# A low-rank adapter's forward pass: one chunk of the input on GpSimd's DMA queue, and the chunks in another order

## The chip, the cores and the metric

The kernel runs on one core of a Trainium2 chip. The metric is the device time of one execution in microseconds, the median of several runs. A profile is one further execution, recorded by the hardware profiler.

## The reference

x has 16 x 2048 = 32,768 rows of 256 numbers in float32. W is 256 x 256, lora_A 256 x 16, lora_B 16 x 256, lora_E has 16 numbers, and scale is 1.0.

```python
x_flat = x.reshape(-1, in_dim)
y = x_flat @ W
lora_out = x_flat @ lora_A
lora_out = lora_out * lora_E
lora_out = lora_out @ lora_B
y = y + scale * lora_out
```

The input and the output have 33.55 MB each; the weights together have 0.3 MB.

## The kernel before, in words

**One weight.** The two paths have the same input, so the kernel first builds one weight, weff = W + (lora_A * lora_E * scale) @ lora_B, and then does y = x @ weff in bfloat16 with sums in float32. TensorE transposes lora_A with an identity that GpSimd builds (L111 to L117), VectorE casts lora_B (L121) and scales the transposed lora_A by lora_E (L129), TensorE multiplies the two (L134), and VectorE adds W and rounds (L138).

**Chunks.** The 256 rows that each of the 128 partitions gets are cut into nine chunks, by PLAN: five of 32 rows per partition, two of 16, two of 32. A chunk of 32 is 4 MB. In each chunk a partition's rows lie one behind another in memory, so that a partition's part of a chunk of 32 is one run of 32 KB. Chunks lie in six slots of SBUF (`slots`), and the output of a chunk overwrites its input.

**Work on a chunk.** It goes by groups of four rows per partition, 64 groups in all. VectorE casts two groups at once to bfloat16 (`rounded`, L148), TensorE transposes eight 128 x 128 blocks per group (`transposed`, L162), VectorE copies the transposed blocks from PSUM (`copied`, L154), TensorE multiplies them by weff (`multiplied`, L173), and ScalarE copies the product back into the slot (L201). TensorE's instructions stand in a loop of four groups per turn; the other engines' instructions are written out.

**Queues.** SP issues W, then the loads of the first six chunks (LEAD = 6), 22 MB. ACT issues lora_A, lora_B and lora_E. All this stands in one critical section, at whose end the engines meet in a barrier. After it SP issues a store whenever a chunk's last group has been copied. Behind store 2 (AFTER) it issues loads 6, 7 and 8, each of which waits until the store that frees its slot (0, 1 or 2) has landed. Then the stores 3 to 8 follow. GpSimd issues no DMA.

**Semaphores.** `Count` keeps a semaphore and the number that has been added to it. A DMA adds 16 when it has landed in full. At the end of the kernel each semaphore is waited for and set back (`spent`), SP's last wait being for the stores.

Of the kernel before, what the change touches and what calls it, by code (L numbers as in the profile page):

```python
# [3 lines left out]

PLAN = [32] * 5 + [16, 16, 32, 32]
ROWS, SLOTS = 32, 6
LEAD = 6
AFTER = {2: [6, 7, 8]}

G, ROUND = 4, 4  # L10

B_PARTS = [(0, 16)]
P = 128
FP32 = mybir.dt.float32
BF16 = mybir.dt.bfloat16
# [15 lines left out]
def kernel(tc, x, W, lora_A, lora_B, lora_E, scale, out):  # L31
    nc = tc.nc
    x_flat = x.flatten_outer_dims()
# [4 lines left out]
    KC = K // P  # L38
    assert K == M and sum(PLAN) * P == N
    starts = [sum(PLAN[:i]) * P for i in range(len(PLAN))]  # L40

    groups = [(i, r) for i, b in enumerate(PLAN) for r in range(0, b, G)]
    NG = len(groups)
    assert NG % ROUND == 0

    def rows_of(flat, i):
        b, r0 = PLAN[i], starts[i]
        return flat[r0:r0 + b * P, :].rearrange("(p b) k -> p b k", b=b)

    def sbuf(name, shape, dt):  # L50
        return nc.alloc_sbuf_tensor(name, shape, dt).ap()
# [6 lines left out]
    e_sb = sbuf("e_sb", [R, 1], FP32)  # L58
# [9 lines left out]
    b_sb = xb[1][:R, G:G + 2, :].rearrange("p g k -> p (g k)").bitcast(FP32)  # L68
# [4 lines left out]
    ps_aeb = psum("ps_aeb", [P, KC, M], FP32)  # L73

    s_w, s_a, s_b, s_e = (Count(nc, f"s_{k}") for k in "wabe")
    s_ld = [Count(nc, f"s_ld{i}") for i in range(len(PLAN))]
    s_st = [Count(nc, f"s_st{i}") for i in range(len(PLAN))]
    s_id, s_set, s_v, s_t, s_m, s_y = (
# [5 lines left out]
    def slot(i):  # L84
        return slots[i % SLOTS][:, :PLAN[i], :]

    def load(i):
        s_ld[i].by(nc.sync.dma_start(out=slot(i), in_=rows_of(x_flat, i)), 16)
# [4 lines left out]
    def spent(engine, count):  # L93
        engine.wait_ge(count.sem, count.total).then_inc(count.sem, -count.total)
# [5 lines left out]
    with tc.tile_critical(no_gpsimd_drain=True):  # L100
        s_w.by(nc.sync.dma_start(out=w_sb, in_=W.rearrange("(c p) m -> p c m", p=P)), 16)
        s_a.by(nc.scalar.dma_start(out=a_sb, in_=lora_A.rearrange("(c p) r -> p c r", p=P)), 16)
        for lo, hi in B_PARTS:
            s_b.by(nc.scalar.dma_start(out=b_sb[lo:hi, :], in_=lora_B[lo:hi, :]), 16)
        s_e.by(nc.scalar.dma_start(out=e_sb, in_=lora_E[:, None]), 16)
        for i in range(LEAD):
            load(i)
    tc.close()
    tc.compile()  # L109
# [4 lines left out]
        out=ident, in_=ident, compare_op=mybir.AluOpType.not_equal, fill=1.0, base=0,  # L114
# [3 lines left out]


    nc.vector.wait_ge(s_b.sem, s_b.total)  # L120
    s_v.by(nc.vector.tensor_copy(out=b_bf, in_=b_sb))  # L121
    nc.tensor.wait_ge(s_a.sem, 16)
    nc.tensor.wait_ge(s_id.sem, 3)
    for c in range(KC):
# [5 lines left out]
        out=ate, in0=ps_at, scalar1=e_sb, scalar2=float(scale),  # L130
# [11 lines left out]
    def rounded(t):  # L142
        i, r = groups[2 * t]
        if r == 0:
            nc.vector.wait_ge(s_ld[i].sem, 16)
        if t >= 2:
            nc.vector.wait_ge(s_t.sem, 2 * t - 2)
        nc.vector.tensor_copy(out=xb[t % 2], in_=slot(i)[:, r:r + 2 * G, :]).then_inc(can_t, 1)  # L148
# [19 lines left out]
    def multiplied(k):  # L168
# [7 lines left out]
        done.then_inc(s_m.sem, 1)  # L176

    rounded(0)
    nc.vector.wait_ge(s_v.sem, 3)
    rounded(1)  # L180
    nc.scalar.sem_inc(can_y, 2)
    for t in range(NG // 2):
        copied(2 * t)
        copied(2 * t + 1)
        if t + 2 < NG // 2:
            rounded(t + 2)
# [35 lines left out]
    nc.tensor.wait_ge(can_y, 1).then_inc(can_y, -1)  # L222
    for count in [s_y] + s_st:
        spent(nc.sync, count)


# [33 lines left out]
```

## Time and profile before

| | us |
|---|---|
| median of 3 runs | 164.19 (164.1 to 164.44) |
| the profiled execution's own time | 164.33 |
| its span, first to last instruction | 162.9 |
| PE busy | 92.5 |
| DVE busy | 79.5 |
| ACT busy | 66.1 |
| POOL busy | 1.0 |
| first store issued | 29.80 |
| last store issued | 130.9 |

The DMA engines moved 67.45 MB, 414 GB/s over the span. In the page, "DMA" and "GB/s" cut the span into 40 slices of 4.07 us; a digit 9 is a share of 90% or more. In a table of stretches, a line begins with the stretch (us from the span's start) and its length, then come each engine's busy time and number of instructions, the granted TensorE clock, the DMA engines' mean share, and the rate. A packet is the part of a DMA that one engine moves in one piece; here a partition's run of 32 KB is one packet. Landing is the moment when all the parts of a DMA are in their place and the semaphore has its full count.

### The profile page before, as it was taken

To read this page: it belongs to the slowest core of one execution; us is meant where nothing else is said; L and a number is where in the kernel's file an instruction comes from. 1 tells how busy PE (TensorE), PEld (TensorE's weight loads), DVE (VectorE), ACT (ScalarE), POOL (GpSimd) and SP (SyncE) were. 2 spreads that over 40 slices of the span, in tenths; PEclk is the share of its full clock that TensorE was granted. 3 is DMA by queue.
4 is the path that set the end of the run, shared out by engine and by line. 5 is a ranking of instruction groups with operands and counts; after the bars stand their busy time and mean duration, and the time that the engine had idled before them with its cause. 6 is when DMAs were issued, how large, how long until landed. Compare 5 with 4: busy or idle time off the path is not lost. (4 is left out here: it accounts for less than half of the span.)

```text
span 162.9 us, 2599 instructions
## 1 busy us (share of the span) xinstructions
PE 92.5 (57%) x1028; PEld 81.5 (50%) x1028; DVE 79.5 (49%) x99; ACT 66.1 (41%) x65; POOL 1.0 (1%) x7
## 2 busy tenths in 40 slices
PE   0112999999999999997000049599999800000000
PEld 0002789888988898896000038498889600000000
DVE  0025878898889888882000083588987300000000
ACT  0300277777777777777000004467777710000000
POOL 0100000000000000000000000000000000000000
PEclk9999999999999999999855556999999965555555
DMA  6999899999998999999999999999999999999991
GB/s 197 390 491 410 386 507 394 394 499 394 426 469 382 326 451 418 467 402 442 442 394 426 467 402 467 420 426 459 410 442 426 410 404 438 451 442 426 442 451 64
DMA packets 3205, 67.45 MB, mean 414 GB/s; under 512 B 625, under 2 KB 897, under 8 KB 897
## 3 DMA queue, kind: packets, MB, share of 16 engines
q1 hardware_dynamic: 2864, 67.37, 97.1%
q10 hardware_dynamic: 336, 0.03, 0.2%
q8 instruction: 1, 0.02, 0.0%
q14 instruction: 4, 0.02, 0.0%
HBM read 33.85 MB, written 33.55 MB: 414 GB/s over the span
## 5 line engine op out<-in xcount | busy, mean ns | idle before, releaser
L201 ACT COPY xy<-psum_y 128x1024 f32<-128x1024 f32 x64 | 64.8, 1012 | 59.3 <-PE psum_y L173 59.3
L173 PE MATMUL psum_y<-weff,xt 128*128 128x256 bf16 x512 | 68.7, 279 | 23.1 <-PEq L97 21.6
L173 PEld LDWEIGHTS psum_y<-weff,xt 128*128 128x128 bf16 x512 | 47.5, 99 | 31.2 <-issue 25.7
L154 DVE COPY xt<-psum_xt 128x1024 bf16<-128x1024 bf16 x64 | 43.8, 687 | 15.3 <-PE psum_xt L162 15.1
L148 DVE CAST xb<-xy 128x2048 bf16<-128x2048 f32 x32 | 38.9, 1218 | 24.0 <-DMA xy<-in_x_dram 24.0
L162 PE MATMUL psum_xt<-ident_bf,xb 128*128 128x128 bf16 x512 | 40.5, 224 | 5.1 <-PEq L97 5.1
L162 PEld LDWEIGHTS psum_xt<-ident_bf,xb 128*128 128x128 bf16 x512 | 35.4, 101 | 7.2 <-issue 5.5
L125 PE MATMUL ps_at<-ident,a_sb 128*16 128x128 f32 x2 | 0.6, 394 | 6.7 <-POOL ident_bf L117 6.7
L121 DVE CAST b_bf<-xb 16x256 bf16<-16x256 f32 x1 | 0.3, 282 | 6.7 <-DMA xb<-in_lora_B_dram 6.7
L201 ACT ACT_TABLE_LOAD x1 | 1.3, 1283 | 5.5 <-PEq L109 5.5
L125 PEld LDWEIGHTS ps_at<-ident,a_sb 128*16 128x16 f32 x2 | 0.1, 88 | 6.7 <-issue 6.7
L134 PE MATMUL ps_aeb<-b_bf,ate 16*128 16x256 bf16 x2 | 0.6, 404 | 2.4 <-DVE ate L129 2.4
L134 PEld LDWEIGHTS ps_aeb<-b_bf,ate 16*128 16x128 bf16 x2 | 0.1, 106 | 2.9 <-DVE ate L129 2.9
L129 DVE TENSOR_SCALAR ate<-ps_at,e_sb 16x256 bf16<-16x256 f32 x1 | 0.5, 471 | 2.2 <-DMA e_sb<-in_lora_E_dram 2.2
L138 DVE TENSOR_TENSOR weff<-xb,ps_aeb 128x512 bf16<-128x512 f32 x1 | 0.7, 687 | 0.8 <-PE ps_aeb L134 0.8
L113 POOL TENSOR_SCALAR_AFFINE_SELECT ident<-ident 128x128 f32<-128x128 f32 x1 | 0.3, 292 | 0.2 <-POOL ident L111 0.2
L117 POOL CAST ident_bf<-ident 128x128 bf16<-128x128 f32 x1 | 0.3, 291 | 0.1
L111 POOL MEMSET ident<- 128x128 f32 x1 | 0.2, 204 | 5.0 <-POOLq L109 5.0
L241 POOL MEMSET const-bfloat16-1.0<- 128x1 bf16 x1 | 0.1, 101 | 0.0
L241 POOL MEMSET const-uint8-127<- 128x1 uint8 x1 | 0.1, 101 | 0.0
L241 POOL MEMSET const-float32-0.0<- 128x1 f32 x1 | 0.1, 98 | 0.2 <-issue 0.2
L241 POOL MEMSET const-float32-1.0<- 128x1 f32 x1 | 0.1, 98 | 0.0
## 6 DMA issues: line engine op xcount, KB each, us to landing
xy<-in_x_dram SPq DMA_DIRECT2D x7, 4096.0 KB, 24.6
out_dram<-xy SPq DMA_DIRECT2D x7, 4096.0 KB, 36.6
xy<-in_x_dram SPq DMA_DIRECT2D x2, 2048.0 KB, 40.1
out_dram<-xy SPq DMA_DIRECT2D x2, 2048.0 KB, 35.9
xb<-in_W_dram SPq DMA_DIRECT2D x1, 256.0 KB, 3.0
a_sb<-in_lora_A_dram ACTq DMA_DIRECT2D x1, 16.0 KB, 3.2
xb<-in_lora_B_dram ACTq DMA_DIRECT2D x1, 16.0 KB, 5.3
e_sb<-in_lora_E_dram ACTq DMA_DIRECT2D x1, 0.1 KB, 7.2
```

The costliest lines, as they stand in the source:

```text
L113: s_id.by(nc.gpsimd.affine_select(out=ident, in_=ident, compare_op=mybir.AluOpType.not_equal, fill=1.0, base=0, pattern=[[-1, P]], channel ...
L117: s_id.by(nc.gpsimd.tensor_copy(out=ident_bf, in_=ident))
L125: at_done = nc.tensor.transpose(ps_at[:, c, :], a_sb[:, c, :], ident)
L129: s_v.by(nc.vector.tensor_scalar(out=ate, in0=ps_at, scalar1=e_sb, scalar2=float(scale), op0=mybir.AluOpType.mult, op1=mybir.AluOpType.mult))
L134: aeb_done = nc.tensor.matmul(ps_aeb[:, c, :], ate[:, c, :], b_bf, start=True, stop=True)
L138: s_v.by(nc.vector.tensor_add(out=weff, in0=w_sb, in1=ps_aeb))
L148: nc.vector.tensor_copy(out=xb[t % 2], in_=slot(i)[:, r:r + 2 * G, :]).then_inc(can_t, 1)
L154: nc.vector.tensor_copy(out=xt[g % 2], in_=ps_xt[g % 2]).then_inc(can_m, 1)
L162: done = nc.tensor.transpose(ps_xt[k % 2][:, j, c, :], xb[k // 2 % 2][:, k % 2 * G + j, c * P:(c + 1) * P], ident_bf)
L173: done = nc.tensor.matmul(ps_y[k % 2][:, j, :], xt[k % 2][:, j, c, :], weff[:, c, :], start=(c == 0), stop=(c == KC - 1))
L201: y = nc.scalar.copy(out=slot(i)[:, r:r + G, :], in_=ps_y[g % 2])
L241: nc = _bacc.Bacc("TRN2", target_bir_lowering=False, num_devices=1)
```

## The change

- PLAN has its first chunk of 16 in front: 16, five times 32, 16, 32, 32. The number of rows is the same.
- The first chunk, 16 rows of 128 partitions, comes by three DMAs. SP loads the first eight rows of all partitions (8 KB of each, 1 MB) and the last eight rows of partitions 120 to 127 (64 KB). GpSimd's queue loads the last eight rows of partitions 0 to 119 (0.98 MB).
- lora_E is loaded in two parts: the first four numbers by GpSimd's queue ahead of its part of x, the other twelve by ACT's queue.
- GpSimd's two DMAs count on one semaphore, `s_sw`. VectorE waits for both before it casts lora_B, and tells GpSimd through `s_seen`, which sets `s_sw` back.
- VectorE's wait for the first chunk asks for the count of SP's two DMAs.
- lora_B, which B_PARTS could split into several DMAs but left in one, is loaded in one DMA, as before.

```diff
-PLAN = [32] * 5 + [16, 16, 32, 32]
+PLAN = [16] + [32] * 5 + [16, 32, 32]
 ROWS, SLOTS = 32, 6
 LEAD = 6
 AFTER = {2: [6, 7, 8]}
...
-B_PARTS = [(0, 16)]
+SW_ROWS, SW_PARTS, E_SW = 8, 120, 4
...
+    s_sw, s_seen = Count(nc, "s_sw"), Count(nc, "s_seen")
...
         s_w.by(nc.sync.dma_start(out=w_sb, in_=W.rearrange("(c p) m -> p c m", p=P)), 16)
         s_a.by(nc.scalar.dma_start(out=a_sb, in_=lora_A.rearrange("(c p) r -> p c r", p=P)), 16)
-        for lo, hi in B_PARTS:
-            s_b.by(nc.scalar.dma_start(out=b_sb[lo:hi, :], in_=lora_B[lo:hi, :]), 16)
-        s_e.by(nc.scalar.dma_start(out=e_sb, in_=lora_E[:, None]), 16)
-        for i in range(LEAD):
+        s_b.by(nc.scalar.dma_start(out=b_sb, in_=lora_B), 16)
+        s_e.by(nc.scalar.dma_start(out=e_sb[E_SW:, :], in_=lora_E[E_SW:, None]), 16)
+        x0, to0, b0 = rows_of(x_flat, 0), slot(0), PLAN[0] - SW_ROWS
+        s_sw.by(nc.gpsimd.dma_start(out=e_sb[:E_SW, :], in_=lora_E[:E_SW, None]), 16)
+        s_sw.by(nc.gpsimd.dma_start(out=to0[:SW_PARTS, b0:, :], in_=x0[:SW_PARTS, b0:, :]), 16)
+        s_ld[0].by(nc.sync.dma_start(out=to0[:, :b0, :], in_=x0[:, :b0, :]), 16)
+        s_ld[0].by(nc.sync.dma_start(out=to0[SW_PARTS:, b0:, :], in_=x0[SW_PARTS:, b0:, :]), 16)
+        for i in range(1, LEAD):
             load(i)
...
     nc.vector.wait_ge(s_b.sem, s_b.total)
+    s_seen.by(nc.vector.wait_ge(s_sw.sem, s_sw.total))
     s_v.by(nc.vector.tensor_copy(out=b_bf, in_=b_sb))
...
         if r == 0:
-            nc.vector.wait_ge(s_ld[i].sem, 16)
+            nc.vector.wait_ge(s_ld[i].sem, 16 if i else s_ld[i].total)
...
     for count in [s_y] + s_st:
         spent(nc.sync, count)
+    spent(nc.gpsimd, s_seen)
+    nc.gpsimd.inc_swdge_sem([s_sw.sem], [s_sw.total], mode="sub")
```

## The prediction

> **What bounds the kernel now.** I read the head of the page first: its DMA rows in 40 slices, then its table of queues.
>
> ```profile
> span 162.9 us, 2599 instructions
> ...
> DMA  6999899999998999999999999999999999999991
> GB/s 197 390 491 410 386 507 394 394 499 394 426 469 382 326 451 418 467 402 442 442 394 426 467 402 467 420 426 459 410 442 426 410 404 438 451 442 426 442 451 64
> ...
> q1 hardware_dynamic: 2864, 67.37, 97.1%
> q10 hardware_dynamic: 336, 0.03, 0.2%
> ```
>
> The sixteen DMA engines are busy from the first slice to the last, while no compute engine is busy for more than 57% of the span. 67.45 MB have to pass, and what passes does so on SP's queue (q1) for 97.1% of sixteen engines' time. So only three things can shorten the run: an earlier first byte, a shorter packet, or a better share-out over the engines. The second view is a table of stretches that I chose; its last two columns are the DMA share and the rate.
>
> ```profile
> 0.00:2.00 2.00, 0.00 (x0) 0.00 (x0) 0.00 (x0) 0.00 (x0) 0.20 (x4) 1.00 0.00 0
> 2.00:3.40 1.40, 0.00 (x0) 0.00 (x0) 0.00 (x0) 0.00 (x0) 0.00 (x0) 1.00 1.27 381
> 3.40:52.00 48.60, 36.90 (x409) 32.23 (x410) 34.22 (x43) 25.57 (x25) 0.79 (x3) 1.00 0.99 427
> 52.00:60.00 8.00, 7.88 (x97) 7.21 (x95) 6.79 (x10) 5.60 (x7) 0.00 (x0) 1.00 1.04 389
> 60.00:157.20 97.20, 47.74 (x527) 42.10 (x525) 38.52 (x48) 34.89 (x35) 0.00 (x0) 0.76 1.01 432
> 157.20:158.40 1.20, 0.00 (x0) 0.00 (x0) 0.00 (x0) 0.00 (x0) 0.00 (x0) 0.50 1.01 437
> 158.40:159.60 1.20, 0.00 (x0) 0.00 (x0) 0.00 (x0) 0.00 (x0) 0.00 (x0) 0.50 0.76 328
> 159.60:160.80 1.20, 0.00 (x0) 0.00 (x0) 0.00 (x0) 0.00 (x0) 0.00 (x0) 0.50 0.19 82
> 160.80:161.30 0.50, 0.00 (x0) 0.00 (x0) 0.00 (x0) 0.00 (x0) 0.00 (x0) 0.50 0.15 66
> 161.30:162.90 1.60, 0.00 (x0) 0.00 (x0) 0.00 (x0) 0.00 (x0) 0.00 (x0) 0.50 0.00 0
> ```
>
> A packet is booked in the stretch where it starts. From 160.80 to 161.30 there are 66 GB/s for 0.5 us, 33 KB: one packet of 32 KB, and nothing starts behind it. So the end is one engine's end. The trace's record of each packet gives the rest: that packet starts at 161.21 and ends at 162.42, 0.5 us ahead of the span's end. The other engines' last packets end at 161.66, 161.21, 161.08, 160.5 and below, the earliest at 159.7. **One engine of sixteen is 0.76 us behind the next and over 2 us behind most.**
>
> Why that one? Packets of 32 KB take 1.213 us in the median everywhere. In two stretches, 58.9 to 77.1 us and 114.0 to 130.9 us, 27 of them take 1.30; linked end to start they follow one another, so each run is one engine's, and by the later links both are the same engine, the one that ends last. It was the first of all to end each load, from 13.1 us (load 0) to 57.7 (load 5), always by about 0.05 us or more, so it was served first from the start. Both stretches are those in which stores run while TensorE still computes. 27 x 0.087 = 2.3 us; 0.5 us more are lost at 89 us. The records have no engine numbers, so which engine it is, no row tells.
>
> The third view, the waits, shows that compute has room.
>
> ```profile
> DVE xb L148 <- DMA xy<-in_x_dram: 24.0, 3, 19.4
> ...
> DVE b_bf L121 <- DMA xb<-in_lora_B_dram: 6.7, 1, 6.7
> PE ps_at L125 <- POOL ident_bf L117: 6.7, 1, 6.7
> ```
>
> VectorE stands 24.0 us waiting for x. The first store is issued at 29.80 us, but SP's queue works on the six first loads until 58 us: whatever delays the beginning of compute by less than 28 us moves no byte. At the end, the last store is issued at 130.9, while the queue ahead of it drains until 153 us: 22 us of room.
>
> **The change part by part.** The sum is made against the profiled execution (164.33 us, span 162.9, so 1.4 around it) and laid on the median of 164.19, 0.14 lower.
>
> *Chunks of 16, 5 x 32, 16, 32, 32.* The same nine loads and stores' bytes; the lead is 22 MB as before. Stores 0 to 2, behind which loads 6 to 8 wait, are 10 MB instead of 12. Load 6 waits for store 0 (about 63 us instead of 69.3), with stores 1 and 2, 8 MB or 19 us, still queued: the queue does not run dry. Then load 8 lands near 107 us instead of 113, and compute ends sooner. Cost 0; the cover is the room of 22 us at the end. If the queue did run dry, each us would count in full.
>
> *First chunk by two queues.* Row counts: 128 partitions over sixteen engines are 8 each (a load of 4 MB lands every 9.71 us, 8 x 1.213). 120 partitions are not 8 each on sixteen: they are 8 on fifteen and none on one, or a flatter split. Other splits (eight engines with 15, or eight with 8 and eight with 7) would relieve all a little or some a lot; I take fifteen times 8, the nearest to the share shown. One engine is then relieved of 8 packets of 8 KB. A packet of 8 KB took 0.309 us (instruction queue, 47.3 us): 2.47 us off. The eight partitions left go by SP, at best one packet on each of eight engines, 0.31 us (at worst all on one, 2.47). First-chunk packets are halved in size: 2 x 0.309 instead of 0.611, 8 times, +0.06 us on each engine. The new completion writes are 9 ns each: nothing.
>
> [...]
>
> *lora_E in two parts.* 12 numbers by ACT's queue, 4 by GpSimd's. Its row is a landing 7.2 us after issue, two packets' turns behind x. Hidden by the 28 us.
>
> *GpSimd issues two DMAs* ahead of the critical section's barrier. No row prices it: SP's six issues took 2.96 us, 0.49 each, as a lower end; an upper end is 5 us for both, the whole time for which POOL now idles before L111. The identity (5.46 to 6.54) and the transposes of lora_A move by as much. Taken: 2 us. Hidden by the 28 us.
>
> *DVE waits for s_sw before b_bf.* Queued behind it are b_bf, ate, weff and the first cast; PE's L134 and all of compute wait for them. If the GpSimd queue gets half of each engine, its 64 KB take 4.9 us from about 3.5: s_sw near 9, weff 4.4 us (6.73 to 11.11) later at the latest, 13.4, against 14.03 for the first cast now. Next comes load 1, at about 18.5. No cost.
>
> *End.* The wait and the subtraction on POOL lie at about 9 us, long done. No row prices what GpSimd's queue adds around the span: 0 to the 0.49 us of one issue; taken 0.
>
> **Sum:** if the relieved engine is the last one, its end goes from 162.42 to about 160.0, and the next, 161.66, sets the end: -0.76, +0.06, and +0.31 if that one is among the eight. That is -0.70 or -0.39; taken -0.55. **164.19 - 0.55 = 163.6 us.**
>
> **The rivals.**
> - *A, forecast: the gap falls on the last engine.* 163.6, own range 163.3 to 163.9. For it: one share of 2.47 us covers all of its lag; and an engine that is served first from the start stands at an end of the order in which packets are handed out, where a row of eights with one place too few has its gap. Against: the gap may be at the other end, or inside.
> - *B, it falls on another, and the last engine is not among the eight:* +0.06, 164.25. The same time comes out if the split is flat. [...]
> - *C, slower: the last engine is among the eight.* +0.31 +0.06: 164.56. For it: if the eight short rows go to the engines that are served first, this one is among them. It decides as soon as that engine is not the one left out.
> - *D, slower: two queues feeding the same engines cost all of them.* In 52 to 60 us, where the stream turns from loads to stores, the rate is 389 instead of 434 GB/s: (434 - 389)/434 x 8 = 0.83 us lost on every engine. If the first 4 MB, read by two queues, lose as much, 165.0; beyond 0.3 us of loss the change is slower even with half of A's gain.
> - *E, GpSimd's packets come later than 28 us:* the stores wait. Nothing speaks for it; over 166.
>
> **How the numbers follow.** What a measurement of this kernel can tell is about 0.2%, 0.33 us. A 0.44, B 0.12, C 0.22, D 0.16, E and others 0.06. A has so much because only two places of sixteen, the ends of the order, compete for the gap by the argument above, and C gets what that argument leaves; it is the weakest step here. Faster: A, 0.44. Same: B and a quarter of C, 0.18 in round numbers. Slower: the rest, 0.38. The range 163.1 to 165.0 reaches from A with half of the third engine's lag recovered (161.21 instead of 161.66) to D. Where A holds, its own range is the one given.
>
> **What would show it.** A right: after the end of the full rate the last stretches hold fewer lone packets, the span falls by 0.4 to 0.8, the 1.30 us packets remain in two stretches. B or C: again one lone packet some 0.8 us behind the others, span equal or 0.3 up. D: a rate well below 420 GB/s between 3.4 and 12 us. First store near 21 us; load 6 issued near 63 us; POOL's identity later than 5.46. What would make it wrong: an end set by something other than the last store's landing, or packets that are slow on another engine this time.

## The result: slower by 3.7%

The changed kernel takes 170.33 us in the median (169.76 to 170.89) against 164.25 us. The ratio is 1.037, 95% interval 1.033 to 1.041. The forecast was 163.6 us, with a range up to 165.0: the time lies 5.3 us above the range, and on the other side of the kernel before.

The profiled execution of the changed kernel took 169.76 us, with a span of 168.4 (162.9 before). The head of its page and its table of queues:

```profile
span 168.4 us, 2607 instructions
...
DMA  5999999999999999999999999999999898999980
GB/s 155 349 315 292 315 395 413 452 397 459 405 467 405 459 387 467 417 436 436 428 397 448 455 413 452 399 475 389 475 389 483 378 481 382 483 393 459 413 374 39
...
q1 hardware_dynamic: 2880, 66.39, 94.6%
q0 software_dynamic: 176, 0.98, 1.9%
```

The DMA engines are as busy as before, and they move less: slices 2 to 5 show 349, 315, 292 and 315 GB/s, where the kernel before had 390, 491, 410 and 386. q0 is GpSimd's queue with its 0.98 MB. A table of stretches of the same execution (the last two columns are DMA share and rate) puts the loss in one place:

```profile
3.40:8.00 4.60, 0.00 (x0) 0.00 (x0) 0.00 (x0) 0.00 (x0) 0.00 (x0) 1.00 1.18 359
8.00:12.00 4.00, 0.00 (x0) 0.00 (x0) 0.00 (x0) 0.00 (x0) 0.00 (x0) 1.00 0.96 293
12.00:16.00 4.00, 0.00 (x0) 0.00 (x0) 0.00 (x0) 0.00 (x0) 0.00 (x0) 1.00 1.05 319
16.00:20.00 4.00, 0.00 (x0) 0.00 (x0) 0.00 (x0) 0.00 (x0) 0.00 (x0) 1.00 0.97 303
20.00:24.00 4.00, 0.00 (x0) 0.00 (x0) 0.00 (x0) 0.00 (x0) 0.00 (x0) 1.00 0.97 356
24.00:28.00 4.00, 1.19 (x4) 0.25 (x4) 0.75 (x2) 1.28 (x1) 0.78 (x3) 1.00 0.95 410
...
162.00:164.00 2.00, 0.00 (x0) 0.00 (x0) 0.00 (x0) 0.00 (x0) 0.00 (x0) 0.50 0.65 279
164.00:166.00 2.00, 0.00 (x0) 0.00 (x0) 0.00 (x0) 0.00 (x0) 0.00 (x0) 0.50 0.19 82
166.00:168.40 2.40, 0.00 (x0) 0.00 (x0) 0.00 (x0) 0.00 (x0) 0.00 (x0) 0.50 0.03 14
```

From 8 to 20 us some 300 GB/s pass, where the kernel before had some 430. The packet records show the same from within: between 8 and 20 us SP's packets of 32 KB take 1.70 to 1.78 us in the mean instead of 1.21, as long as packets of q0 are served, which is from 5.9 to 22.2 us. After that they take 1.22 again.

Where the 5.5 us of span went can be read from the landings of the sixteen parts of each DMA. Take the eighth of the sixteen as "most engines". Most engines end the last store 4.2 us later than before (164.5 against 160.3). They already ended the 22 MB of first loads about 4.4 us later (62.8 against 58.4). And the last engine is 3.8 us behind most, instead of 2.6: another 1.2 us.

The landings also show the gap. One engine ends load 1 at 21.2 us, the next at 23.7, and it stays 2.1 us ahead of all others to the end (162.13 against 164.20). The lead is near the 2.47 us of eight packets of 8 KB, so I take it for the engine that the 120 partitions left out. It isn't the last one.

Compute began late. Of the waits of the changed kernel:

```profile
DVE b_bf L129 <- PEq L116: 25.0, 1, 25.0
...
POOL ident L118 <- POOLq L116: 22.2, 1, 22.2
```

GpSimd's issues took 0.64 and 0.54 us and were over at 2.7 us, but POOL passed the barrier behind the critical section only after its DMAs had landed (24.06 us), and all other engines waited there for it. The first store was issued at 39.86 us instead of 29.80.

### The profile page after: what moved, and what is told of

Read it like the earlier page. It is cut to its first block, busy times and chain, and to the rows that moved or that the text cites. A ratio compares the mean times of both kernels' runs of the same rounds, so it can differ in the third digit from the quotient of the medians.

```text
span 168.4 us, 2607 instructions
## 1 busy us (share of the span) xinstructions
PE 94.4 (56%) x1028; PEld 83.0 (49%) x1028; DVE 79.4 (47%) x99; ACT 66.1 (39%) x65; POOL 2.2 (1%) x9
## 5 line engine op out<-in xcount | busy, mean ns | idle before, releaser
L181 PE MATMUL psum_y<-weff,xt 128*128 128x256 bf16 x512 | 70.0, 282 | 8.7 <-PEq L100 7.1
L181 PEld LDWEIGHTS psum_y<-weff,xt 128*128 128x128 bf16 x512 | 48.3, 101 | 17.2 <-issue 11.3
L162 DVE COPY xt<-psum_xt 128x1024 bf16<-128x1024 bf16 x64 | 43.8, 687 | 17.2 <-PE psum_xt L170 17.0
L170 PE MATMUL psum_xt<-ident_bf,xb 128*128 128x128 bf16 x512 | 41.4, 228 | 2.1 <-PEq L100 2.1
L170 PEld LDWEIGHTS psum_xt<-ident_bf,xb 128*128 128x128 bf16 x512 | 36.1, 102 | 4.3 <-issue 2.5
L109 POOL DMA_DIRECT2D e_sb<-in_lora_E_dram x1 | 0.6, 639 | 1.0 <-PEq L116 1.0
L110 POOL DMA_DIRECT2D xy<-in_x_dram x1 | 0.5, 538 | 0.0
L118 POOL MEMSET ident<- 128x128 f32 x1 | 0.2, 204 | 22.2 <-POOLq L116 22.2
```

Of the source, the lines that this page charges most:

```text
L109: s_sw.by(nc.gpsimd.dma_start(out=e_sb[:E_SW, :], in_=lora_E[:E_SW, None]), 16)
L110: s_sw.by(nc.gpsimd.dma_start(out=to0[:SW_PARTS, b0:, :], in_=x0[:SW_PARTS, b0:, :]), 16)
L162: nc.vector.tensor_copy(out=xt[g % 2], in_=ps_xt[g % 2]).then_inc(can_m, 1)
L170: done = nc.tensor.transpose(ps_xt[k % 2][:, j, c, :], xb[k // 2 % 2][:, k % 2 * G + j, c * P:(c + 1) * P], ident_bf)
L181: done = nc.tensor.matmul(ps_y[k % 2][:, j, :], xt[k % 2][:, j, c, :], weff[:, c, :], start=(c == 0), stop=(c == KC - 1))
```

## The experiments

Three things are new at once: the order of the chunks, a second queue that carries x, and pieces of another shape. The theories, as the expectations name them: R, the order; Q, GpSimd's queue; P, any two queues or two packet sizes side by side; S, the shape. Ratios are against the kernel before on the same chip.

**The order alone, and GpSimd's queue with lora_E alone.**

```diff
 (kernel before)
-PLAN = [32] * 5 + [16, 16, 32, 32]
+PLAN = [16] + [32] * 5 + [16, 32, 32]
```

> The kernel before with the new order of chunks alone; everything is loaded by SP and ACT as before. Theory Q (GpSimd's queue: as long as packets of GpSimd's queue are being served, the whole stream falls from about 430 to 300 GB/s): 164.0 to 164.6 us, and the full rate from 4 us on. Theory P (any two queues with packets of 8 KB and 32 KB side by side): the same. Theory R (the new order of chunks reads x in a pattern that is slow): 168 us or more, with about 300 GB/s between 6 and 22 us.

Measured: 164.23 us, ratio 1.000 (0.999 to 1.001); 442 GB/s from 8 to 12 us. R falls. The order costs and gives nothing.

```diff
 (changed kernel)
-s_sw.by(nc.gpsimd.dma_start(out=to0[:SW_PARTS, b0:, :], in_=x0[:SW_PARTS, b0:, :]), 16)
-s_ld[0].by(nc.sync.dma_start(out=to0[:, :b0, :], in_=x0[:, :b0, :]), 16)
-s_ld[0].by(nc.sync.dma_start(out=to0[SW_PARTS:, b0:, :], in_=x0[SW_PARTS:, b0:, :]), 16)
+s_ld[0].by(nc.sync.dma_start(out=to0, in_=x0), 16)
```

> The changed kernel with the whole first chunk on SP; GpSimd's queue carries only four numbers of lora_E. Theory Q: no packets of GpSimd's queue after 6 us, so no slow stage: 164.0 to 164.6 us, the engines' barrier passed before 9 us. If instead the use of GpSimd's queue costs by itself, however little it carries: 166 us or more, and a late barrier.

Measured: 164.22 us, ratio 1.000 (0.999 to 1.001). GpSimd's four numbers landed at 7.6 us and the barrier was passed about 8.5. The use of the queue costs nothing by itself.

**The same piece on ACT's queue.** The 120 partitions go from GpSimd's queue to ACT's, all of lora_E too.

```diff
-s_sw.by(nc.gpsimd.dma_start(out=to0[:SW_PARTS, b0:, :], in_=x0[:SW_PARTS, b0:, :]), 16)
+s_sw.by(nc.scalar.dma_start(out=to0[:SW_PARTS, b0:, :], in_=x0[:SW_PARTS, b0:, :]), 16)
```

> The changed kernel with the 120-partition part of the first chunk on ACT's queue instead of GpSimd's (all of lora_E on ACT too). Theory Q: no slow stage, 163.6 to 164.6 us; one engine ends its loads 2.1 to 2.5 us ahead of the others, as in the changed kernel. Theory P: the slow stage stays, 167 to 170 us. If the engine left out is the one that ends last, up to 0.8 us under the kernel before; if not, 0 to 0.4 us over it.

Measured: 171.06 us, ratio 1.043 (1.038 to 1.048). Q falls. The rates in this kernel's page, slice by slice, are even a little lower than with GpSimd's queue, down to 290:

```profile
GB/s 148 332 294 290 309 321 433 433 433 433 433 433 433 433 389 437 453 441 418 449 389 460 414 456 402 464 402 464 387 472 395 468 389 426 433 480 387 480 364 46
```

**Half the bytes in as many packets.**

```diff
-SW_ROWS, SW_PARTS, E_SW = 8, 120, 4
+SW_ROWS, SW_PARTS, E_SW = 4, 120, 4
```

> The changed kernel with four rows instead of eight on GpSimd's queue: the same 120 packets, 4 KB each, half the bytes. In the changed kernel each engine served one packet of GpSimd's queue in turn with one 32 KB packet of SP's, eight turns, to 22 us. If the length of the slow stage goes by turns, it still ends near 21 us and the time is 169 to 170.5 us. If it goes by bytes, it ends near 14 us and the loss halves: 167 to 168 us.

Measured: 166.58 us, ratio 1.014 (1.012 to 1.017). Both expectations missed: the last of GpSimd's packets of x ended at 17.2 us, and the loss was 2.3 us instead of 6.1, even under half. With as many turns and half the bytes, more than half of the loss is gone, so the price does not go by the turns that the packets take with SP's. Up to here P was my likeliest theory.

What did not fit P was the engine in the gap. It had no x from GpSimd's queue, yet its own eight packets of load 1 took 1.80 us each in the mean (6.2 to 20.6 us). Something shared was slow; what it is, no record shows. What sets the 120-partition piece apart from the loads whose packets of 32 KB take 1.21 us is its shape: it goes into 120 partitions instead of 128. Theory S: such a piece is slow by itself and slows what moves beside it, whatever the queue and the size of the packets.

**All 128 partitions of the eight rows on GpSimd's queue.** Two queues, packets of 8 KB beside 32 KB, a late barrier: all that remains. The shape is full, and the third piece of the first chunk (64 KB into eight partitions, on SP's queue) is gone with it. By theory S I expected no loss, 164.0 to 164.8 us.

```diff
-SW_ROWS, SW_PARTS, E_SW = 8, 120, 4
+SW_ROWS, SW_PARTS, E_SW = 8, 128, 4
...
-s_ld[0].by(nc.sync.dma_start(out=to0[SW_PARTS:, b0:, :], in_=x0[SW_PARTS:, b0:, :]), 16)
```

> The changed kernel with all 128 partitions of the eight rows on GpSimd's queue, and no third piece on SP. [...] Theory P (two queues, or packets of two sizes, side by side): the slow stage stays, 168 us or more, and the barrier is passed late in both.

Measured: 164.49 us, ratio 1.001 (1.000 to 1.002). The stretches and a wait of this kernel:

```profile
3.40:8.00 4.60, 0.00 (x0) 0.00 (x0) 0.00 (x0) 0.00 (x0) 0.00 (x0) 1.00 1.16 471
8.00:12.00 4.00, 0.00 (x0) 0.00 (x0) 0.00 (x0) 0.00 (x0) 0.00 (x0) 1.00 0.90 387
12.00:16.00 4.00, 0.00 (x0) 0.00 (x0) 0.00 (x0) 0.00 (x0) 0.00 (x0) 1.00 1.06 457
16.00:20.00 4.00, 0.00 (x0) 0.00 (x0) 0.00 (x0) 0.00 (x0) 0.00 (x0) 1.00 1.06 453
```
```profile
POOL ident L117 <- POOLq L115: 17.4, 1, 17.4
```

GpSimd's packets of 8 KB took 0.31 us, SP's 1.21, side by side until 18.6 us. The loss is gone, and P with it. (A packet counts where it starts, so the 387 stands between a high stretch and two others.) This run also prices the late compute: the barrier was passed at about 20 us instead of 5.5, and the time is at most 0.2% longer.

**The three pieces on one queue.** The pieces of the changed kernel, all issued by SP. By theory S I expected the loss to stay, 166 to 168 us.

```diff
-s_sw.by(nc.gpsimd.dma_start(out=to0[:SW_PARTS, b0:, :], in_=x0[:SW_PARTS, b0:, :]), 16)
+s_sw.by(nc.sync.dma_start(out=to0[:SW_PARTS, b0:, :], in_=x0[:SW_PARTS, b0:, :]), 16)
```

> The changed kernel's three pieces of the first chunk, all on SP's queue; lora_E on ACT. [...] Theory P: one queue, so no loss: 164.0 to 164.8 us.

Measured: 167.41 us, ratio 1.018 (1.016 to 1.020). No second queue, and the rate falls to 228 GB/s while the piece is moved, where the kernel with the order of chunks alone had 402; from 4 to 9 us its packets took some 0.6 us instead of 0.31:

```profile
3.40:8.00 4.60, 0.00 (x0) 0.00 (x0) 0.00 (x0) 0.31 (x1) 0.20 (x1) 1.00 1.04 228
8.00:12.00 4.00, 1.19 (x4) 0.25 (x4) 1.23 (x3) 0.97 (x1) 0.58 (x2) 1.00 1.36 395
12.00:16.00 4.00, 0.99 (x10) 1.02 (x11) 2.49 (x3) 0.00 (x0) 0.00 (x0) 1.00 0.69 295
```

So the piece is slow by itself, as theory S has it. The third line shows that the loss does not end with the piece. The 64 KB into eight partitions come later on the same queue, and they are a narrow transfer too. Beside and just behind them, from 11.2 to 13.9 us, fifteen packets of load 1 took 2.1 to 2.4 us. In the kernel with 128 partitions on GpSimd's queue and in the one with the whole first chunk on SP, the first sixteen took 1.21. The difference is 0.9 us per engine in the mean, so the 3.1 us are not the 120 partitions' alone. The changed kernel has this piece as well.

**The same addresses in HBM, other partitions in SBUF.** A slow read in HBM could still be the cause, since the 120-partition piece also reads in another pattern. So the kernel before got one DMA more, 16 packets of 32 KB. Two kernels differ in its destination alone: partitions 0 to 15 of the sixth slot in the first, every eighth partition in the second. By theory S I expected a loss in both, and by my estimate a larger one in the first, 168 us or more.

```diff
 (kernel before; the second kernel has slots[5][0:P:8, :, :])
+        s_ex.by(nc.scalar.dma_start(out=slots[5][:16, :, :], in_=x_flat[:512, :].rearrange("(p b) k -> p b k", b=32)), 16)
-        for i in range(LEAD):
+        for i in range(LEAD - 1):
             load(i)
+        nc.sync.wait_ge(s_ex.sem, 16)
+        load(LEAD - 1)
```

> The kernel before with one DMA more: 512 KB of x, sixteen runs of 32 KB, on ACT's queue into partitions 0 to 15 of the sixth slot, ahead of the slot's own load, which waits for it (the data are not used). Every engine has one packet more, 1.21 us of work. [...] Theory P or a cause on the HBM side: the same as with the partitions spread out, to 0.3 us.

> [...] Theory S: a loss beyond the 1.2 us, about 2 us, less than with partitions 0 to 15: 166.5 to 168 us. Theory P or a cause on the HBM side: as with partitions 0 to 15.

Measured: 169.29 us for partitions 0 to 15, ratio 1.029 (1.027 to 1.031), and 166.95 us for every eighth partition, ratio 1.015 (1.013 to 1.017). The two stretches in which the extra DMA is moved, for each kernel:

```profile
8.00:12.00 4.00, 0.00 (x0) 0.00 (x0) 0.00 (x0) 0.00 (x0) 0.00 (x0) 1.00 1.29 262
12.00:16.00 4.00, 0.00 (x0) 0.00 (x0) 0.00 (x0) 0.00 (x0) 0.00 (x0) 1.00 0.66 139
```
```profile
8.00:12.00 4.00, 0.00 (x0) 0.00 (x0) 0.00 (x0) 0.00 (x0) 0.00 (x0) 1.00 1.10 328
12.00:16.00 4.00, 0.00 (x0) 0.00 (x0) 0.02 (x1) 0.00 (x0) 0.06 (x1) 1.00 0.87 352
```

The first pair of lines is partitions 0 to 15, the second every eighth. The extra packets took 3.95 us in the mean (3.2 to 4.7) in the first and 2.26 us (2.0 to 2.5) in the second, against 1.21 for a packet of that size in a full-width load. That is 3.3 and 1.9 times as long; why, no run shows. HBM addresses, packets and queue are equal, so the difference of 2.3 us comes from the partitions. Less the 1.2 us of its own work (one packet for each engine, an estimate from 16 packets and 16 engines), the extra DMA costs 3.7 and 1.4 us. SP waits for it ahead of the barrier, so compute begins late in both, at 18.3 and 16.0 us; by the 128-partition run, where the barrier was passed at 20 us, that costs at most 0.2%. No run varies the destination of the 120-partition piece alone; that its loss has the same cause rests on the 128-partition run and on its packets of 0.6 us, 1.9 times 0.31, as those into every eighth partition are 1.9 times 1.21.

**112 partitions.** 112 is sixteen times seven, so each of the sixteen engines can have seven packets and none is left out: an estimate from the count, as the records name no engine. First with GpSimd's queue, then on SP alone.

```diff
-SW_ROWS, SW_PARTS, E_SW = 8, 120, 4
+SW_ROWS, SW_PARTS, E_SW = 8, 112, 4
```

> The changed kernel with 112 instead of 120 partitions on GpSimd's queue and the other sixteen on SP. [...] Theory S: 112 foreign packets of 8 KB beside SP's stream, 7 per engine, nearly the 120 of the changed kernel: 168 to 170 us. If the uneven share (fifteen engines of sixteen) were the cause: no loss, 164 to 165 us.

> The 112-partition split with all three pieces on SP's queue. [...] Theory S: a loss well under that of the 120-partition piece on one queue (2 to 3 us): 164.6 to 166 us. [...]

Measured: 168.6 us, ratio 1.028 (1.023 to 1.032), and 166.05 us, ratio 1.011 (1.007 to 1.016). If the packets are shared out evenly here, the uneven share is not the cause: the loss is still 4.2 us. On one queue 112 partitions cost 1.6 us where 120 cost 3.1, and the rate falls less while the piece is moved:

```profile
3.40:8.00 4.60, 0.32 (x2) 0.12 (x2) 0.28 (x1) 1.28 (x1) 0.79 (x3) 1.00 1.02 324
8.00:12.00 4.00, 0.86 (x4) 0.13 (x2) 1.17 (x3) 0.00 (x0) 0.00 (x0) 1.00 1.17 363
```

The smaller loss is what I expected, and the time lies at the upper edge of it; why 112 partitions cost less than 120 is not shown. Here the piece on SP goes into sixteen partitions, and the first sixteen packets of load 1 took 1.5 to 2.6 us, 1.0 us more than 1.21 in the mean. So a good part of the 1.6 us is that piece's.

**Why one engine is late at the end.** The kernel before without the compute of chunks 3 to 8; their slots are stored as loaded. Loads and stores are the same.

```diff
 (kernel before)
+    groups = [g for g in groups if g[0] < 3]
     NG = len(groups)
...
+    for i in range(3, len(PLAN)):
+        nc.sync.wait_ge(s_ld[i].sem, 16)
+        store(i)
```

> The kernel before with the casts, transposes, products and copies of chunks 3 to 8 left out: their slots are stored as loaded (so these chunks of the output are x, not y). Loads and stores are the same, in the same order; compute is over near 46 us, before the first store moves. If packets of 1.30 us come from stores running beside compute: none is left and the last engine ends within 0.5 us of the next; 163 to 163.9 us. If they belong to that engine's stores alone: as before, 164.0 to 164.5 us.

Measured: 163.37 us, ratio 0.994 (0.992 to 0.996). The two runs of 1.30 us packets are gone. The last engine is still 0.7 us behind the next (162.17 against 161.49), a little more than expected: single long packets are left (1.9 us behind an instruction fetch at 47 us, 2.1 us at 110 us). Behind most engines it is 2.2 us, against 2.6 in the kernel before, so one engine is late without the slow runs too. Stores that run beside compute do slow one engine, by 0.09 us per packet of 32 KB; through what, is open.

## Why the prediction was wrong

**The step that failed is "First chunk by two queues".** It counted the piece as work of the engines alone: 8 packets of 0.309 us less on one engine, 0.06 us more on each, 0.31 on eight. Its durations came from full-width loads and from a packet of the instruction queue, and it took them over to a transfer of another shape. The packets themselves took 0.39 us in the steady part, which is near. What the step left out is that SP's packets beside them went from 1.21 to 1.7 us, on all sixteen engines. The term written as +0.06 us measured about +4.2 us on most engines. The 0.31 us for the eight partitions left on SP was too small as well: in the one-queue kernel packets on nearly every engine were some 0.9 us longer beside that piece. The rows of the kernel before held no transfer of such a shape, so the price had to be bounded; I bounded the number of packets and not their duration. In the runs the duration goes with the destination: a packet of 32 KB took 3.95 us in the mean into partitions 0 to 15, 2.26 into every eighth partition, and 1.21 in a full-width load. What makes it so is not shown.

**Rival D named the place and not the mechanism.** It said that two queues on the same engines would cost all of them, with a low rate between 3.4 and 12 us, by up to 0.83 us, and had a chance of 0.16. The sign was right, and so was the place where the low rate begins; it lasted to 22 us. The size was five times too small, and the reason was wrong: two queues cost nothing (128 partitions: ratio 1.001), and the same three pieces on one queue cost 3.1 us.

**A and C: where the gap falls.** The split was as taken: one engine without a part, 2.1 us ahead of the others. In the one-queue kernel the semaphore of the 120-partition DMA shows it too: it rose once at 2.1 us, and fifteen times from 8.8 to 9.9. But it was not the last engine, so A did not happen; the argument from the order of service did not hold. That order was also read too firmly: the lead of the first engine at the end of a load shrank from 0.11 us (load 0) to 0.01 (load 5). And 161.21 is the end of the last engine's own packet before its last, so the third engine ended at 161.08 (and the earliest at 159.4). That moves the lower end of the range a little, and not the sum. Had A happened, 0.76 us would have been won and 4.2 lost. C can't be told apart: the last engine is 1.2 us further behind, and most of this has another source. Its slow packets were 31 of 32 KB and 8 of 16 KB instead of 27: 31 x 0.09 + 8 x 0.045 - 2.35 = 0.8 us. Compute began later and ran longer beside stores. That this makes such packets slow is what the last experiment bears out. The remaining 0.4 us may be single long packets, which differ from run to run; that is not shown.

**The late begin.** I expected s_sw near 9 us and the first store near 21; they came at 24.1 and 39.9. The steps had GpSimd's queue getting half of each engine. It got one packet of 8 KB for each packet of 32 KB of SP's: eight turns of 2 us. And I did not see that POOL would hold the barrier until its DMAs had landed. The cover of 28 us that I named was enough all the same: with the barrier at 20 us and the full shape, the time moved by 0.1% (0.0 to 0.2). What it did not cover is the 0.8 us above.

**What held.** The order of chunks costs nothing (1.000). DMA bounds the kernel, and one engine sets the end. A version faster than the kernel before did not come out of this: the lag to be won by taking load from the last engine is 0.76 us, and the four forms tried with 120 partitions cost 2.3 to 6.8 us.

## What to carry to other kernels

In this kernel a DMA over fewer than 128 partitions was not a smaller copy of the full one. Each of the narrow shapes tried was slower than its bytes: with 120 partitions a packet of 8 KB took some 0.6 us on one queue instead of 0.31, with 112 the rate fell to 324 GB/s, and into 16 partitions a packet of 32 KB took 3.95 or 2.26 us instead of 1.21. They slowed the full-width stream as well, on nearly every engine (1.7 us per packet instead of 1.21 in the changed kernel). A remainder of 64 KB in eight partitions was not free either: some 0.9 us more per engine beside it. Where DMA is the bound, try large transfers over 128 partitions first, cut along the free dimension (ratio 1.001 here, against 1.037 with 120 partitions); where a balance over engines tempts, measure the shape alone first. When a price is taken from a row, ask what shape that row has, not only what size.

## What the runs showed of the hardware that I had not expected

- 16 packets of 32 KB into partitions 0 to 15 take 3.95 us in the mean, into every eighth partition 2.26 us, where full-width loads take 1.21. The rate of all queues falls from 430 GB/s to 262 and 139 in the two stretches, or to 328 and 352.
- An engine with no part in the narrow transfer is slowed too: 1.80 us per packet in the mean instead of 1.21.
- The narrow pieces cost more with the 120 partitions beside the stream, on GpSimd's queue (6.1 us), than with all pieces ahead of it on one queue (3.1 us).
- POOL passed the barrier of the critical section only after its own DMAs had landed (24.06 us, 19.3 and 7.6 us in three kernels; its next instruction came 0.8 us later each time), so a slow DMA of GpSimd's held every engine.
- Stores beside compute slow one engine's packets by 7% (1.30 us instead of 1.213); without that compute the kernel is 0.6% faster.
